# Routing in a mixture-of-experts layer: the first expert's rows picked with the one-hot matrix as loaded operand, row numbers and gates formed in another order

## The chip, the core and the metric

The kernel runs on one core of a Trainium2 chip. Its engines are PE (matrix products), DVE (VectorE), ACT (ScalarE), POOL (GpSimd) and SP, which here only issues DMAs. The metric is the device time of one execution in microseconds. The profile comes from one such execution.

## The reference

It is an encoder of two layers over 512 tokens of 1024 features. Each layer has an attention mixer and then a mixture of 16 experts of which a router picks 2 for each token. What matters here is the end of the mixer and the start of the experts:

```python
h = layer_norm(DEEPNORM_ALPHA * h + mix, ln1_g[l], ln1_b[l])        # mix = o @ w_out[l]
...
scores = sigmoid(einsum('nd,de->ne', h, router_w))                  # 512 x 16
biased = (scores + router_bias).reshape(n, N_GROUPS, GROUP_SIZE)
group_sel = argmax(sum(top_k(biased, 2)[0], -1), -1)                # best of 4 groups
_, idx = top_k(where(in_group, biased, NEG_INF), 2)                 # 2 experts of that group
gates = sel / sum(sel, -1)
for e in range(N_EXPERTS):
    a = silu(h @ w_gate[e]) * (h @ w_up[e])
    y = y + dense_gates[:, e:e + 1] * (a @ w_down[e])
h = layer_norm(DEEPNORM_ALPHA * h + y, ln2_g[l], ln2_b[l])
```

## The kernel before

The 512 tokens are four tiles of 128 rows, `h[:, t]`. Weights stream in as pieces of 128x1024 (512 KB) that SP's queue loads in a fixed order (L324) as buffers come free. Most pieces are split into a rounded high part, made by ACT (L369), and a low part, made by DVE (L376) or POOL (L378). A product is then three matmuls (L400 to L402: high x high, low x high, high x low). The first piece of each expert matrix is kept whole and multiplied in full f32 (L1700), which the trace records as two PE rows for each matmul. `prep` makes high parts ahead of need as far as `prep_limit` and the buffer budget allow; `prep_low` makes the low parts.

`w_out_phase` ends the mixer. For each tile t it forms two halves of the output projection (`mm(t, 0)`, `mm(t, 1)`), which DVE adds to h out of PSUM (L1375). `stats` takes the sums: a square on ACT (L729), and POOL raises the variance to a power (L736). `tr` turns h by PE transposes (L1384), copied out by ACT and DVE (L1387). `logits` is 8 products with the router's 16 columns (L1396). `score` applies the norm to the logits afterwards (L1400, L1401) and ACT takes a tanh. `finish` makes the normed rows themselves, on DVE alone (L1407, L1408: `fast`) or on DVE and POOL (L1410 to L1412), and SP writes them to `hD` in DRAM. FIN = 13 makes tiles 0, 2 and 3 fast.

`choose(a, b)` finds the two experts of tiles a to b-1: a chain of some 14 short DVE instructions (L1502 to L1523). `places(a, b)` counts with small matmuls (L1532) which row of its expert each token takes, and DVE writes that number into `R1` (L1534). Rows of the experts from the second on are fetched from `hD` by an indirect DMA (L1619) at row numbers that `start(e)` forms from one-hots (L1587) and small matmuls (L1594).

The first expert's rows are not fetched. `pick(t)` makes a 128x128 one-hot of the tile (L1418) and multiplies: the loaded operand is a strided view of h (every eighth column), the moving operand the one-hot, and the result lands already transposed in two PSUM tiles `G`. `trans_x(0)` then only splits `G` into high and low parts (L1658 to L1660). `zero` opens and closes the sums in `G` with a product of zeros (L1424). `moe` follows with `proj(0, "g")` (the first expert's gate matrix), `start(1)`, `make_gates` (L1539 to L1549), `proj(0, "u")` and `trans_x(1)` (L1689), and so on for 16 experts.

Each engine runs its instructions in one order that a scheduler sets when the kernel is built, with semaphores between engines. `issue_after(i)` puts what is issued under it behind the instruction i on the same engine. `busy(n)` issues n small matmuls of zeros that nobody reads (L552), "dummies" below.

## Time and profile before

| | us |
|---|---|
| Median of 3 runs | 1386.37 |
| Lowest and highest of them | 1381.67, 1392.21 |
| The profiled execution's own time | 1383.48 |
| Its span, first to last instruction | 1381.7 |
| Mean granted PE clock, share of full speed | 0.978 |

The span is 1.8 us less than the execution's own time; that remainder lies around the instructions. The profiled execution lies 2.9 us under the median. The two layers run the same code, so each place of interest stands twice in the trace: at about 305 to 364 us and at about 968 to 1024 us.

### The profile page before, as it was taken

Reading aid. Unit: us, or ns where it says so; the run is one execution under the profiler, and the core shown is the slowest. Engines: PE = TensorE matmul, PEld = TensorE weight load, DVE = VectorE, ACT = ScalarE, POOL = GpSimd, SP = SyncE. Lnnn points to the kernel's source line nnn. Section 1 sums busy time; section 2 is a strip of 40 time slices with the busy share of each in tenths; the row PEclk is TensorE's granted clock in tenths of the full one; section 3 lists DMA queues with packets and bytes.
Section 4 is the critical chain, followed back from the end, with each engine's and each line's share of the span. In section 5 each row is a group of like instructions: output and inputs, shape, how many; then the busy total and the mean of one; then the engine's idle time right before and its main releaser. Section 6 shows DMA issues by size and latency. Waiting matters only on the chain. (4 is left out here: it accounts for less than half of the span.)

```text
span 1381.7 us, 18726 instructions
## 1 busy us (share of the span) xinstructions
PE 1295.2 (94%) x6034; PEld 959.4 (69%) x6042; DVE 1017.1 (74%) x2292; ACT 799.4 (58%) x1429; POOL 265.0 (19%) x204
## 2 busy tenths in 40 slices
PE   8999999989999999899799989999999999979994
PEld 4786666768777776577588766677877777656773
DVE  6668888676678777677755788867858877757775
ACT  5468756651566665566436776557246666555662
POOL 1012222342021210111000222214412111102110
PEclk9999999998999999999999999999999999999998
DMA  8311313257699998999610124224769999888991
GB/s 258 87 46 31 111 62 92 80 174 242 232 301 316 348 364 244 342 390 357 228 43 16 31 81 123 93 76 155 233 242 296 312 356 352 251 290 295 387 367 61
DMA packets 114969, 289.01 MB, mean 209 GB/s; under 512 B 20548, under 2 KB 43332, under 8 KB 114864
## 3 DMA queue, kind: packets, MB, share of 16 engines
q1 hardware_dynamic: 101740, 253.48, 52.3%
q0 software_dynamic: 11008, 31.36, 9.1%
q10 hardware_dynamic: 2116, 2.89, 0.7%
q8 instruction: 50, 0.82, 0.2%
q14 instruction: 55, 0.45, 0.1%
HBM read 267.09 MB, written 27.00 MB: 213 GB/s over the span
## 5 line engine op out<-in xcount | busy, mean ns | idle before, releaser
L369 ACT ACTIVATE slot<-arena 128x1024 fp32r<-128x1024 f32 (+3 forms) x147 | 127.5, 887 | 95.7 <-PE A L402 27.3
L376 DVE TENSOR_TENSOR slot<-slot,slot 128x1024 fp32r<-128x1024 f32 x105 | 128.2, 1224 | 60.8 <-ACT slot L369 58.0
L369 ACT ACTIVATE slot<-slot 128x1024 fp32r<-128x1024 f32 x111 | 117.2, 1059 | 95.5 <-PE A L402 35.9
L402 PE MATMUL S<-slot,rounded 128*128 128x512 f32 x368 | 148.5, 404 | 0.3 <-DVE slot L376 0.2
L402 PE MATMUL A<-slot,rounded 128*128 128x512 f32 x372 | 147.2, 396 | 0.0
L376 DVE TENSOR_TENSOR slot<-arena,slot 128x1024 fp32r<-128x1024 f32 (+2 forms) x101 | 112.7, 1120 | 39.2 <-ACT slot L369 36.6
L400 PE MATMUL S<-slot,rounded 128*128 128x512 f32 x316 | 137.0, 436 | 3.7 <-ACT rounded L771 1.3
L401 PE MATMUL S<-slot,rounded 128*128 128x512 f32 x316 | 125.8, 398 | 1.0 <-DVE rounded L1926 0.7
L400 PE MATMUL A<-slot,rounded 128*128 128x512 f32 x288 | 125.6, 436 | 1.0 <-ACT rounded L771 1.0
L1624 POOL DMA_INDIRECT yD<-arena,ix x28 | 46.9, 1674 | 406.4 <-ACT rounded L1659 194.8
L401 PE MATMUL A<-slot,rounded 128*128 128x512 f32 x288 | 114.0, 396 | 2.3 <-DVE rounded L772 2.3
L2042 ACT ACTIVATE arena<-arena,ast 128x256 f32<-128x256 f32 (+3 forms) x160 | 88.9, 557 | 34.7 <-DVE ast L2031 25.5
L378 POOL TENSOR_TENSOR slot<-arena,slot 128x1024 fp32r<-128x1024 f32 (+4 forms) x46 | 70.2, 1542 | 195.7 <-ACT slot L369 175.1
L369 ACT ACTIVATE rounded<-slot 128x1024 fp32r<-128x1024 f32 x70 | 74.1, 1059 | 45.8 <-PE A L401 25.5
L400 PE MATMUL S<-rounded,slot 128*128 128x512 f32 (+1 forms) x224 | 89.3, 400 | 0.0
L401 PE MATMUL S<-rounded,slot 128*128 128x512 f32 (+1 forms) x224 | 88.4, 395 | 0.0
L402 PE MATMUL S<-rounded,slot 128*128 128x512 f32 (+1 forms) x224 | 88.1, 393 | 0.0
L402 PEld LDWEIGHTS S<-slot,rounded 128*128 128x128 f32 x368 | 70.7, 192 | 16.7 <-DVE slot L376 1.1
L2073 ACT ACTIVATE slot<-T 128x128 fp32r<-128x128 f32 (+3 forms) x128 | 53.4, 431 | 48.6 <-PE T L2068 47.7
L402 PEld LDWEIGHTS A<-slot,rounded 128*128 128x128 f32 x372 | 70.6, 190 | 15.4
L1700 PE MATMUL A<-slot,arena 128*128 128x512 f32 x168 | 79.4, 594 | 0.5 <-ACT arena L1658 0.5
L400 PEld LDWEIGHTS S<-slot,rounded 128*128 128x128 f32 x316 | 60.6, 192 | 21.7 <-issue 2.9
(371 smaller groups left out, 3061.8 us busy)
## 6 DMA issues: line engine op xcount, KB each, us to landing
slot<-in_exp_w_down_dram SPq DMA_DIRECT2D x80, 512.0 KB
slot<-in_exp_w_up_dram SPq DMA_DIRECT2D x73, 512.0 KB
slot<-in_exp_w_gate_dram SPq DMA_DIRECT2D x72, 512.0 KB
arena<-in_exp_w_gate_dram SPq DMA_DIRECT2D x60, 512.0 KB
arena<-in_exp_w_up_dram SPq DMA_DIRECT2D x59, 512.0 KB
arena<-in_exp_w_down_dram SPq DMA_DIRECT2D x52, 512.0 KB
arena<-in_w_in_dram SPq DMA_DIRECT2D x14, 512.0 KB
slot<-in_w_in_dram SPq DMA_DIRECT2D x12, 512.0 KB
```

The lines of the kernel that those rows point to most:

```text
L369: self.nc.scalar.activation(hi, r, AF.Copy)
L376: self.nc.vector.tensor_sub(lo, r, hi.bitcast(F32))
L378: self.nc.gpsimd.tensor_tensor(lo, r, hi.bitcast(F32), OP.subtract)
L400: t.matmul(ps, xh, wh, start=start, stop=False)
L401: t.matmul(ps, xl, wh, start=False, stop=False)
L402: t.matmul(ps, xh, wl, start=False, stop=stop)
L1624: self.nc.gpsimd.indirect_dma_start(out=self.yD[:, :], out_offset=bass.IndirectOffsetOnAxis(ap=ix[:, 0:1], axis=0), in_=y, in_offset=None, ...
L1700: nc.tensor.matmul(ps, xW(e)[:, kk], P.raw.f[:, 512 * k:512 * k + 512], start=kk == 0, stop=kk == 7)
L2042: nc.scalar.activation(p, p, AF.Exp, bias=self.st[:, m:m + 1], scale=-1.0, accum_out=self.st[:, 2 + m:3 + m])
L2073: nc.scalar.activation(self.part(0), self.ps, AF.Copy)
```

## The change

- `pick(t)`: the one-hot is now the loaded operand, and the contiguous row of h (two halves of 512) moves; two matmuls for each tile in place of eight. The result is the picked rows, not turned. `zero` is gone. `trans_x(0)` therefore copies the two tiles `G` to SBUF (ACT and DVE) and turns them by 8 PE transposes like those of any other expert, and then splits.
- `choose`, `places` and `pick` take tiles 0 to 2 in one go, tile 3 apart. `centre(3)`, the first half of the last `finish`, stands ahead of that, the second half behind the choice of tile 3.
- `finish(0)` is issued behind the copy of tile 1's transposes; before, it stood ahead of that tile's sums.
- No expert weight is split during `w_out_phase` (`prep_limit`), and low parts are held back (`hold_low`) until `G` is copied; the first expert's splits thus move from the end of the attention to the routing and the first gate.
- `start(1)`, which forms the second expert's row numbers, stands ahead of `trans_x(0)`, and `make_gates` between the two halves of the first gate projection.
- 3 dummies stand between the last tile's transposes and 13 behind its logits.

```diff
+WARM5 = 3
+WARM6 = 13
...
     def prep_low(self, n):
+        if self.hold_low:
+            return
         while self.i_low < n:
...
+        self.prep_limit = max(ids) + 1
         P = [self.get(i) for i in ids]
...
+        def centre(t):
+            z = self.h[:, t]
+            v.scalar_tensor_tensor(z, z, st[t][:, 1:2], self.lnrow[0], op0=OP.add, op1=OP.mult)
...
-        def pick(t, ks=range(8)):
+        def pick(t):
             oh = ho.f[:, 128 * t:128 * (t + 1)]
-            if ks[0] == 0:
-                v.tensor_scalar(oh, self.biota, self.R1[:, t, 0:1], None, op0=OP.is_equal)
-            hk = self.h[:, t].rearrange("p (d k) -> p k d", k=8)
-            for k in ks:
-                nc.tensor.matmul(self.G[k // 4][:, 128 * (k % 4):128 * (k % 4 + 1)], hk[:, k], oh, start=False, stop=False)
-
-        def zero(g, start):
-            nc.tensor.matmul(self.G[g], self.bzero, self.cum3, start=start, stop=not start)
+            v.tensor_scalar(oh, self.biota, self.R1[:, t, 0:1], None, op0=OP.is_equal)
+            for n in range(2):
+                i = nc.tensor.matmul(self.G[n], oh, self.h[:, t, 512 * n:512 * n + 512], start=t == 0, stop=t == NT - 1)
+            return i
...
                 if t == 1:
-                    finish(0, FIN & 1)
-                finish(t, FIN >> t & 1)
-            if t == 2:
-                self.choose(0, 2)
-        self.choose(2, 3)
+                    with self.tc.issue_after(self.i_trv.ins):
+                        finish(0, True)
+                finish(t, t == 2)
...
         tr(3, 0)
-        for g in range(2):
-            zero(g, True)
-        self.places(0, 2)
+        with self.tc.issue_after(self.i_tr.ins):
+            self.busy(WARM5, True)
         tr(3, 1)
-        pick(0, range(4))
-        pick(0, range(4, 8))
         scored(3)
-        finish(3, FIN >> 3 & 1)
-        pick(1)
+        with self.tc.issue_after(self.i_logit.ins):
+            self.busy(WARM6, True)
+        self.choose(0, 3)
+        centre(3)
+        self.places(0, 3)
+        for t in range(3):
+            pick(t)
         self.choose(3, 4)
-        self.places(2, 3)
-        pick(2, range(4))
         self.places(3, 4)
-        pick(2, range(4, 8))
+        with self.tc.issue_after(self.i_chosen.ins):
+            finish(3, True)
...
-        with self.tc.issue_after(self.i_chosen.ins):
+        self.prep_limit, self.hold_low = len(self.pieces), True
+        with self.tc.issue_after(self.i_score.ins):
             self.prep()
-        for g in range(2):
-            pick(3, range(4 * g, 4 * g + 4))
-            zero(g, False)
+        pick(3)
...
             if e == 0:
-                for half, ps in enumerate(self.G):
-                    hi, lo = [xT(0, s)[:, 4 * half:4 * half + 4] for s in range(2)]
-                    i = parts(ps.rearrange("p (k n) -> p k n", k=4), None if half else xW(0), hi, lo)
-                return i
+                x = B(gb[0]).f
+                nc.scalar.activation(x[:, 0:512], self.G[0], AF.Copy)
+                i = v.tensor_copy(x[:, 512:1024], self.G[1])
+                self.hold_low = False
+                with self.tc.issue_after(i.ins):
+                    self.prep_low(self.idx[l, "g0", WG] + 1)
+                self.hold_low = True
...
+        start(1)
         i_x = trans_x(0)
         pg[0] = self.psA.tile([128, 512], F32, name="A")
         proj(0, "g", pg[0], 0, 2)
         with self.tc.issue_after(i_x.ins):
-            start(1)
+            self.make_gates()
...
         with self.tc.issue_after(i_x.ins):
-            self.make_gates()
             gt[1] = self.slot_gates(self.slots(1, ohs.pop(1)))
```

Line numbers of the changed kernel run up to 14 higher than those used here. Three places of the built order follow, in the first layer; the second layer has the same ones.

**First place.** POOL at the end of the attention, before: three low parts of the first expert (L378), then the powers (L736) of tiles 0 and 1, with a low part of the attention's output (L1328) between them.

```order
L378 TENSOR_TENSOR slot8_2817<-arena_77,rounded_78 128x1024
L378 TENSOR_TENSOR slot14_2825<-arena_77,slot3_2824 128x1024
L378 TENSOR_TENSOR slot4_2820<-arena_77,slot1_2819 128x1024
L736 TENSOR_TENSOR bst_2861<-bst_2861,mhalf_82 128x1
L1328 TENSOR_TENSOR rounded_78<-slot5_1010,rounded_78 128x256
L736 TENSOR_TENSOR bst_2919<-bst_2919,mhalf_82 128x1
L1411 TENSOR_TENSOR h_73<-h_73,arena_77 128x1024
```


POOL at the same place now (L741 is the power, L1333 the attention's low part):

```order
L1333 TENSOR_TENSOR rounded_78<-slot5_1010,rounded_78 128x256 x2
L741 TENSOR_TENSOR bst_2847<-bst_2847,mhalf_82 128x1
L1333 TENSOR_TENSOR rounded_78<-slot5_1010,rounded_78 128x256
L741 TENSOR_TENSOR bst_2905<-bst_2905,mhalf_82 128x1
L1422 TENSOR_TENSOR h_73<-h_73,arena_77 128x1024
```


The three splits ahead of the first power are gone from POOL. DVE there, before: L1407 and L1408 are `finish(0)`, L1375 adds the second half of tile 1 to h, L1400 and L1401 are the scores of tile 0, and L1387 copies transposes of tile 0 (first row) and tile 1 (last row).

```order
L1387 COPY arena_77<-T_2887 128x512
L735 TENSOR_SCALAR bst_2861<-bst_2861 128x1
L1407 SCALAR_TENSOR_TENSOR h_73<-h_73,bst_2861,arena_77 128x1024
L1408 SCALAR_TENSOR_TENSOR h_73<-h_73,bst_2861,arena_77 128x1024
L1375 SCALAR_TENSOR_TENSOR h_73,zsum_2815<-S_2893,h_73 128x512
L1400 SCALAR_TENSOR_TENSOR sc_2816<-gbrw_2226,bst_2861,T_2907 128x16
L721 TENSOR_TENSOR bst_2919<-zsum_2815 128x1
L1401 SCALAR_TENSOR_TENSOR sc_2816<-sc_2816,bst_2861,gbrw_2226 128x16
L723 TENSOR_SCALAR bst_2919<-bst_2919 128x1
L1387 COPY arena_77<-T_2931 128x512
```


DVE there now (L1381 adds to h, L1406 and L1407 are the scores, L1412 and L1419 `finish(0)`):

```order
L1393 COPY arena_77<-T_2873 128x512
L1381 SCALAR_TENSOR_TENSOR h_73,zsum_2815<-S_2879,h_73 128x512
L1406 SCALAR_TENSOR_TENSOR sc_2816<-gbrw_2226,bst_2847,T_2893 128x16
L726 TENSOR_TENSOR bst_2905<-zsum_2815 128x1
L1407 SCALAR_TENSOR_TENSOR sc_2816<-sc_2816,bst_2847,gbrw_2226 128x16
L728 TENSOR_SCALAR bst_2905<-bst_2905 128x1
L1393 COPY arena_77<-T_2917 128x512
L1412 SCALAR_TENSOR_TENSOR h_73<-h_73,bst_2847,arena_77 128x1024
L1419 SCALAR_TENSOR_TENSOR h_73<-h_73,bst_2847,arena_77 128x1024
```


`finish(0)`, whose second half waits for POOL's power, moved from ahead of tile 1's addition to behind the copy of its transposes.

**Second place.** PE from the last picks to the first gate, before: L1421 picks, L1424 closes `G`, L1700 is the whole piece of the gate, L400 to L402 the split ones.

```order
L1421 MATMUL A_2832<-arena_77,h_73 128x128 x4
L1421 MATMUL A_2831<-arena_77,h_73 128x128 x4
L1424 LDWEIGHTS b_zero_92
L1424 MATMUL A_2831<-cum3_86,b_zero_92 128x512
L1421 MATMUL A_2832<-arena_77,h_73 128x128 x4
L1424 LDWEIGHTS b_zero_92
L1424 MATMUL A_2832<-cum3_86,b_zero_92 128x512
L1700 MATMUL A_3226<-arena_77 128x512 x2
L400 MATMUL A_3226<-rounded_78 128x512
L401 MATMUL A_3226<-rounded_78 128x512
```


PE there now: L1430 picks tile 3, L1599 are the last of the small matmuls for the second expert's row numbers, L1697 turns the picked rows, L1713 is the whole piece.

```order
L1599 LDWEIGHTS oh_e_3196
L1599 MATMUL T_3200<-mv_444,oh_e_3196 128x8
L1430 MATMUL A_2817<-h_73,arena_77 128x512
L1430 MATMUL A_2818<-h_73,arena_77 128x512
L1599 LDWEIGHTS oh_e_3198
L1599 MATMUL T_3200<-mv_444,oh_e_3198 128x8
L1697 MATMUL T_3218<-cst_72,arena_77 128x128 x4
L1697 MATMUL T_3226<-cst_72,arena_77 128x128 x4
L1713 MATMUL A_3236<-arena_77 128x512 x2
L404 MATMUL A_3236<-rounded_78 128x512
L405 MATMUL A_3236<-rounded_78 128x512
```


Eight transposes stand between the last pick and the gate, and the second expert's row numbers ahead of both.

**Third place.** DVE behind the last one-hot of tile 3, before: L1534 writes the row numbers, L1418 makes the one-hot, L1660 makes the low parts of the picked rows, then one-hots for the second expert (L1587) and the gates (from L1539).

```order
L1534 SCALAR_TENSOR_TENSOR R1_3005<-T_3193,ohs_3006 128x16
L1418 TENSOR_SCALAR arena_77<-b_iota1_436,R1_3005 128x128
L1660 TENSOR_TENSOR rounded_78<-A_2831,rounded_78 128x256
L1660 TENSOR_TENSOR rounded_78<-A_2832,rounded_78 128x512
L1587 TENSOR_SCALAR oh_e_3238<-b_iota1_436,R1_3005 128x128
L1587 TENSOR_SCALAR oh_e_3240<-b_iota1_436,R1_3005 128x128
L1587 TENSOR_SCALAR oh_e_3242<-b_iota1_436,R1_3005 128x128
L1587 TENSOR_SCALAR oh_e_3244<-b_iota1_436,R1_3005 128x128
L1539 TENSOR_SCALAR sc_2816<-sc_2816 128x64
```


DVE there now: L1539 row numbers, L1428 the one-hot, L1592 a one-hot of the second expert, L1688 copies half of `G`, L1604 and L1613 belong to the second expert's row numbers, L380 is a low part of a weight piece, L1665 of the picked rows.

```order
L1539 SCALAR_TENSOR_TENSOR R1_3095<-T_3169,ohs_3096 128x16
L1428 TENSOR_SCALAR arena_77<-b_iota1_436,R1_3095 128x128
L1592 TENSOR_SCALAR oh_e_3198<-b_iota1_436,R1_3095 128x128
L1688 COPY arena_77<-A_2818 128x512
L1604 COPY sw_3205<-T_3200 128x6
L380 TENSOR_TENSOR rounded_78<-arena_77,rounded_78 128x1024
L1613 SCALAR_TENSOR_TENSOR sf_3207<-sw_3205,cst_72 128x1
L1665 TENSOR_TENSOR rounded_78<-T_3218,rounded_78 128x256
L1614 SCALAR_TENSOR_TENSOR ix_3208<-sw_3205,cst_72,sf_3207 128x1
L1665 TENSOR_TENSOR rounded_78<-T_3226,rounded_78 128x512
L380 TENSOR_TENSOR slot4_3184<-arena_77,rounded_78 128x1024
L380 TENSOR_TENSOR slot14_3187<-arena_77,slot3_3186 128x1024
```


The three low parts of the first gate's pieces stand among those of the picked rows now, and the gates behind them.

## Rows read from the trace of the kernel before

**Rows 1.** The page: PE's busy time, share of the span, instructions.

```profile
PE 1295.2 (94%) x6034; PEld 959.4 (69%) x6042; DVE 1017.1 (74%) x2292; ACT 799.4 (58%) x1429; POOL 265.0 (19%) x204
```

**Rows 2.** Windows by stage: busy time (x instructions) of each engine, PEclk, DMA.

```profile
core 0: us, PE busy (x) PEld busy (x) DVE busy (x) ACT busy (x) POOL busy (x), PEclk, DMA share, GB/s
304.77:329.12 24.35, 21.34 (x113) 18.34 (x113) 14.75 (x39) 4.16 (x10) 11.66 (x8) 0.86 0.52 171
329.12:350.61 21.49, 19.91 (x112) 19.32 (x112) 11.52 (x63) 3.63 (x7) 1.50 (x2) 0.92 0.82 288
350.61:363.90 13.29, 12.90 (x61) 8.42 (x60) 11.94 (x50) 6.72 (x7) 3.10 (x3) 1.00 0.65 220
968.45:987.98 19.53, 18.51 (x113) 16.20 (x112) 15.47 (x37) 3.80 (x8) 12.56 (x8) 1.00 0.57 174
987.98:1010.23 22.25, 20.35 (x112) 19.72 (x113) 11.82 (x65) 3.76 (x8) 1.50 (x2) 0.85 0.84 293
1010.23:1024.21 13.98, 12.90 (x62) 8.26 (x60) 12.80 (x51) 7.57 (x8) 4.11 (x3) 1.00 0.66 227
```

**Rows 3.** Timeline of PE, first and second layer: start, busy, [idle before <-releaser].

```profile
311.45 1.10 PE L1384 MATMUL T<-cst,h 128*128 128x128 f32 x4 [3.01 <-DVE sc L1400]
...
972.81 0.72 PE L1384 MATMUL T<-cst,h 128*128 128x128 f32 x4 [1.02 <-DVE sc L1400]
```

**Rows 4.** Windows of two stretches in the first layer.

```profile
310.65:317.40 6.75, 5.95 (x16) 4.88 (x17) 2.97 (x12) 1.37 (x3) 0.56 (x1) 0.50 0.78 277
334.55:337.85 3.30, 3.30 (x19) 3.30 (x17) 3.23 (x11) 0.22 (x1) 0.96 (x1) 0.50 0.71 248
```

**Rows 5.** Timeline of POOL and DVE, first layer.

```profile
302.66 5.73 POOL L378 TENSOR_TENSOR slot<-arena,slot 128x1024 fp32r<-128x1024 f32 x2
...
308.95 1.75 DVE L1408 SCALAR_TENSOR_TENSOR h<-h,bst,arena 128x1024 f32<-128x1024 f32 x1 [2.81 <-POOL bst L736]
```

**Rows 6.** Timeline of PE, first layer, from the last logits to the first gate.

```profile
332.63 1.96 PE L1396 MATMUL T<-rg,arena 128*128 128x16 f32 x16 [0.77 <-DVE R L1534]
...
334.54 4.06 PE L1421 MATMUL A<-arena,h 128*128 128x128 f32 x16
338.44 0.25 PE L1532 MATMUL T<-oh,bones_all 128*128 128x16 bf16 x4
...
338.64 5.96 PE L1421 MATMUL A<-arena,h 128*128 128x128 f32 x24
...
350.61 1.88 PE L1700 MATMUL A<-arena 128*128 128x512 f32 x4
```

**Rows 7.** One line's instructions: min/median/max ns, first and last start.

```profile
L1421 PEld LDWEIGHTS A<-arena,h x128: 312/335/338, 334.5 to 1009.6; 128*128 128x128 f32 x128
```

**Rows 8.** Chain that ended last: start, length, what.

```profile
1271.47 1.72 PE A L1700 x4
```

**Rows 9.** Timeline of PE, first layer: the second expert's transposes; dummies.

```profile
363.90 1.04 PE L1689 MATMUL T<-cst,arena 128*128 128x128 f32 x8
...
681.61 0.65 PE L552 MATMUL A<-mchunk,b_zero 128*1 128x384 bf16 x3
```

**Rows 10.** Timeline of DVE, first layer.

```profile
321.11 1.69 DVE L721 TENSOR_TENSOR bst<-zsum 128x1 f32<-128x1 f32 x1
...
329.40 0.67 DVE L1375 SCALAR_TENSOR_TENSOR h<-S,h 128x512 f32<-128x512 f32 x1
...
334.86 1.28 DVE L1407 SCALAR_TENSOR_TENSOR h<-h,bst,arena 128x1024 f32<-128x1024 f32 x1
...
338.06 0.17 DVE L1502 SCALAR_TENSOR_TENSOR rt<-sc,rb 128x16 f32<-128x16 f32 x1
...
341.04 0.26 DVE L1522 TENSOR_TENSOR oh<-cst,rt 128x16 bf16<-128x16 f32 x2
...
362.27 1.22 DVE L376 TENSOR_TENSOR rounded<-slot,rounded 128x1024 fp32r<-128x1024 f32 x1
```

**Rows 11.** Timeline of PE, second layer: the second expert's transposes.

```profile
1024.21 1.14 PE L1689 MATMUL T<-cst,arena 128*128 128x128 f32 x8 [0.89 <-DMA arena<-hD,ix]
```

More of the change, by code (lines that the diff above doesn't have):

```diff
@@ L546, in setup, with busy @@
         self.pump()
-    def busy(self, n):
-        ps = self.psA.tile([128, 512], F32, name="A")
+    def busy(self, n, small=False):
+        ps = self.psS.tile([128, 512], F32, name="S") if small else self.psA.tile([128, 512], F32, name="A")
         for _ in range(n):
@@ L1406, in finish @@
             if fast:
-                v.scalar_tensor_tensor(z, z, st[t][:, 1:2], self.lnrow[0], op0=OP.add, op1=OP.mult)
+                if t < NT - 1:
+                    centre(t)
                 v.scalar_tensor_tensor(z, z, st[t][:, 4:5], self.lnrow[1], op0=OP.mult, op1=OP.add)
@@ L1690, in trans_x @@
                 hi, lo = [xT(e, s)[:, 4 * half:4 * half + 4] for s in range(2)]
-                parts(ps, None if half else xW(e), hi, lo)
+                i = parts(ps, None if half else xW(e), hi, lo)
+            if e == 0:
+                self.hold_low = False
+                with self.tc.issue_after(i.ins):
+                    self.prep_low(self.i_prep)
+            return i
         def proj(e, c, ps, j0, j1, then=None):
```

9 lines of the change are left out of this document (5 added, 4 removed).

## The prediction

> **What bounds the kernel now.** I read the page first: PE is busy 94% of the span [rows 1], so a change pays where PE is not doing needed work. Then I cut the place of the change into three stages for each layer [rows 2]. Stage A runs from the first logits to the end of the output projection, stage B from the last tile's transposes to the first gate product, stage C from there to the second expert's transposes. They take 24.35, 21.49 and 13.29 us in the first layer, 19.53, 22.25 and 13.98 us in the second. The same instructions stand in both, so the differences are waits and clock.
>
> In stage A the timeline shows one stall in each layer, 3.01 and 1.02 us, in front of tile 1's transposes, which wait for the score of tile 0 [rows 3]. DVE could not give that score: it stood in `finish(0)`, whose second half waited 2.81 us for POOL's power, and POOL was busy for 5.73 us with two weight splits queued ahead of it [rows 5]. Behind the long stall PE's granted clock fell to 0.50, which is 1.2 GHz, for 6.75 us [rows 4]; PE was busy for 5.95 us of those, so some 3.0 us were lost. That accounts for the first layer: 24.35 less 19.53 is 4.8, against 2.0 of longer stall and 3.0 of clock.
>
> In stage B, PE is nearly always busy (19.9 of 21.5 us), and the picks are most of it: the 64 rows from 334.54 to the gate at 350.61 [rows 6]. Their pace is 0.24 us a row at either clock: 16 rows in 3.9 us where the clock was 0.50 [rows 4], 24 in 5.96 where it was full. What sets it is the load of the strided operand, 335 ns [rows 7]. Stage C is PE-bound in the first layer (12.90 of 13.29 us) and loses 0.89 us in the second, waiting for the gather of the second expert's rows [rows 11].
>
> Behind stage C I count every microsecond as kept. PE is the bound there, and SP's queue waits mostly for the splits that free its buffers, so an earlier start shifts the loads as well.
>
> **Stage A.** The three splits leave POOL's queue and `finish(0)` stands behind the score, so neither can hold it. What is late next is PE itself: the second layer without its 1.02 us gives 18.5 us for both. Gain 5.85 + 1.0. A new neighbour is tile 1's `finish`, two products on POOL, under which DVE's short sums for tile 2 now fall. A one-column addition once took 1.69 us [rows 10]. Queued behind such a wait are the copy of tile 2's transposes and the logits on PE. The wait costs between nothing (it ends before PE arrives) and 1.7 us a layer; I take 0.6, since PE has ten matmuls in hand there.
>
> The Trainium skill's page "SBUF — State Buffer", section "Who interferes with whom", says that the one contention on the engines' side is a pair of ports that VectorE and GpSimd share under an exclusive lock. The 1.69 us addition agrees with that; by the rule each of these sums could wait for a whole GpSimd product, which is the upper end already taken.
>
> **Stage B**, counted from the first transposes of tile 3. Transposes, three dummies, transposes: 0.5 + 0.6 + 0.5, half of 1.04 us for 8 [rows 9] and 0.65 for three dummies; the eviction that the second half needs starts at 329.40, takes 0.67 [rows 10] and is over by 1.0. DVE's copy out of PSUM, 0.7, ends at 2.45. The second eight logit rows, half of 1.96 [rows 6], end at 3.5. From the score DVE needs the rest of three tiles' choice. One tile's whole chain took 3.2 us, from 338.06 to the end of the row at 341.04 [rows 10]; its first half is now done ahead of the score, three index searches stand in place of one, and `centre(3)` (1.28) is in it. I take 3.2 again: 6.7. The 13 dummies, 0.2 each, end at 6.1 and cost nothing as long as they end before that. 18 counting matmuls (eight took 0.2 between 338.44 and 338.64 [rows 6]) and their output: 7.4. Row numbers and the first one-hot: 7.9.
>
> A pick is now two f32 matmuls of 512 contiguous columns, with a contiguous load. Two of that form take 1.72 us [rows 8], so three tiles take 5.2: 13.1. Tile 3's choice and `finish(3)` run on DVE meanwhile (3.2 + 1.3 against 5.2). Counting, row number and one-hot of tile 3: 13.8. Its pick: 15.5. PSUM to SBUF, 0.7 + 0.2: 16.4. The new transposes and the eviction that the gate waits for: 1.2, between the 0.9 that 8 transposes take and the 1.6 from 363.90 to the next gate start where ACT was occupied. Stage B is 17.6 us, a gain of 3.9 and 4.65. The sum has eight hand-overs between engines at 0.1 or less each; for those I add back 0.8 a layer, ends 0 and 1.6.
>
> **Stage C.** The work on PE is 12.9 us in both layers [rows 2]. The gather is issued ahead of the gate in place of behind it, so its wait goes. New on DVE are three low parts, 1.22 each [rows 10], among those of the picked rows, with the gates behind them. Added up from the copy of `G` (six splits 7.3, copies and low parts 2.0, gates and row numbers 2.3) that is 11.6 us, and PE asks for the last gate column about 10.9 us after the copy (1.2 to the gate product, 5.9 for it, 3.8 into the up product). The 0.7 that PE may wait stands against small waits of 0.4 in the first layer that go. I take 12.9: gain 0.4 and 1.1. The three splits cost nothing only while PE works on the whole piece and its neighbours; without that cover they cost 3.7 us.
>
> **Clock.** In B, PE now idles for 0.6 us ahead of the counting and 0.5 behind it, with only small matmuls between. Such a stretch made a clock of 0.50 for 3.3 us in the first layer of before [rows 4]. There it cost nothing, since the strided loads set the pace; the new picks are paced by streaming and would lose half of it, 1.7 us. Whether the 13 dummies prevent it no row tells. The ends are 0 and a stretch like the 6.75 us one in each layer, 3.4 us lost in each; I take 1.7 once, in one layer of two.
>
> The Trainium skill's "TensorE: Matmul & The Clock Gate", section "What's actually happening", states that "the default state is throttled, and activity releases the throttle". By that rule the dummies are there for the picks, and the waiting on DVE that this change puts around them speaks against it; the trace agrees as far as the clock did fall behind the 3.01 us stall.
>
> **The sum.** Gains: 5.85 + 1.0 + 3.9 + 4.65 + 0.4 + 1.1 = 16.9 us. Taken back: ports 1.2, hand-overs 1.6, clock 1.7. Net 12.4 us. Against the profiled execution's own 1383.5 that is 1371.1; I say **1371 us**. That execution lies 2.9 us under the median; the stall of A differs from layer to layer, so slower executions may hold more of it, and I don't add the 2.9.
>
> **Rivals.**
> (a) Everything fits: no port wait, no slow stretch, hand-overs hidden. 1383.5 - 16.9 = 1366.6. For it: the dummies. Against it: eight hand-overs in a row.
> (b) DVE becomes the bound of B: three tiles chosen at once take not 3.2 but twice that, since the three finds stand in a row (3.2 us for one tile [rows 10]). PE waits another 3.2 us a layer: 1377.5. For it: DVE has 11.5 us of work in B already [rows 2]. Against it: instructions of three tiles can fill each other's gaps.
> (c) The clock stays at 0.50 through the picks in both layers, 3.4 lost in each: 1371.1 + 5.1 = 1376.2.
> (d) It doesn't do what it says in A: the score is still late, for another reason on DVE. Then A's 6.85 and its 1.2 drop out: 1376.7.
> (e) Slower: the clock falls at the waits behind the logits and stays at 0.50 to the end of the first gate. Paced by it are 13 dummies, four picks (6.9), the new transposes (0.9) and a gate (half of 12.9): 15.3 us lost a layer, 30.6 in all. In place of the 1.7 that gives 1400. It turns the sign when 7 us a layer are lost, 14 us in a row at 0.50; the longest stretch in these places is 6.75.
>
> **How the numbers follow.** The forecast 0.45, (a) 0.20, (b) 0.15, (c) 0.12, (d) 0.05, (e) 0.03. Bounds: 1366.6 at best; 1380 with the clock's 6.8, the ports' 3.4 and hand-overs of 3.2. The runs of before spread from 4.7 below their median to 5.8 above, so I open the lower end to 1363 and leave 1380. About 1% (14 us) is what a measurement of this kernel can tell from no change. Measured from the median that is 1372.5, from the profiled execution 1369.6; (a) lies past both, the forecast between them, so half of it counts. Faster 0.46, within 1% 0.50, slower 0.04.
>
> **What would show it.** Right: no stall ahead of L1390 (the tile transposes) in A; A 18.5 to 19.5 us in both layers; L1430 at 0.43 us a row where the clock is full; B near 18 and C near 13; the gather wait gone. Wrong: PE waiting over 2 us for L1527 or L1428 (rival b); a PEclk of 0.50 over the picks (c, e); a wait ahead of L1390 or L1402 on DVE (d, ports); or time given back in later experts, as waits on loads that I counted as shifted.

## The result

The changed kernel takes 1369.47 us in the median of 4 runs (1366.76 to 1374.33), the kernel before 1388.80 in its 4 (1381.67 to 1392.21). The ratio of the runs is 0.988, 95% interval 0.9858 to 0.9903, so 1.2% less (the two medians alone would give 0.986), where 1371 us and a range of 1363 to 1380 were forecast. The profiled execution took 1368.57 us, with a span of 1366.8, which is 14.9 under the 1381.7 of before.

The page's line of PE for the changed kernel, whose lines are numbered up to 14 higher:

```profile
PE 1285.1 (94%) x5986; PEld 937.6 (69%) x5986; DVE 1019.5 (75%) x2278; ACT 800.0 (59%) x1431; POOL 250.0 (18%) x196
```

The windows of its six stages, cut as in [rows 2]:

```profile
core 0: us, PE busy (x) PEld busy (x) DVE busy (x) ACT busy (x) POOL busy (x), PEclk, DMA share, GB/s
304.76:323.01 18.25, 18.25 (x114) 16.29 (x113) 12.59 (x31) 3.88 (x9) 6.80 (x4) 1.00 0.39 121
323.01:340.99 17.98, 15.24 (x89) 8.81 (x87) 13.17 (x64) 5.92 (x10) 1.50 (x2) 1.00 0.93 337
340.99:354.12 13.13, 12.78 (x56) 8.43 (x57) 12.20 (x37) 7.81 (x9) 1.94 (x1) 1.00 0.93 317
957.76:976.01 18.25, 18.25 (x113) 16.29 (x112) 12.59 (x31) 3.88 (x9) 6.81 (x4) 1.00 0.44 147
976.01:994.20 18.19, 15.26 (x90) 8.82 (x88) 13.18 (x64) 5.93 (x10) 1.51 (x2) 1.00 0.85 303
994.20:1007.33 13.13, 12.79 (x56) 8.43 (x57) 12.19 (x37) 7.78 (x9) 2.01 (x1) 1.00 0.93 329
```

Against [rows 2], A gains 6.10 and 1.28 us, B 3.51 and 4.06, C 0.16 and 0.85: 15.96 in all. PE is busy for the whole of A, and its clock is full in all six rows. Between the first layer's C and the second layer's A the changed kernel is 0.91 us shorter (603.64 for 604.55), behind the second C 1.98 longer (359.47 to the end for 357.49): 15.96 + 0.91 - 1.98 = 14.9.

PE in stage B of the first layer, from its timeline (start, busy, [idle before <-releaser]); L1402 are logits, L557 dummies, L1537 the counting, L1430 picks, L1697 the transposes of the picked rows, L1713 the gate:

```profile
324.73 2.01 PE L1402 MATMUL T<-rg,arena 128*128 128x16 f32 x16
326.67 2.27 PE L557 MATMUL S<-mchunk,b_zero 128*1 128x384 bf16 x13
329.70 0.18 PE L1537 MATMUL T<-oh,b_tri 128*128 128x16 bf16 x1 [0.76 <-DVE oh L1527]
...
330.90 5.42 PE L1430 MATMUL A<-h,arena 128*128 128x512 f32 x12 [0.54 <-DVE arena L1428]
...
336.98 1.98 PE L1430 MATMUL A<-h,arena 128*128 128x512 f32 x4 [0.55 <-DVE arena L1428]
...
339.83 1.13 PE L1697 MATMUL T<-cst,arena 128*128 128x128 f32 x8 [0.87 <-DVE sw L1604]
```

Three tiles are picked in 5.25 us, from 330.90 to the next product at 336.15, 0.44 a row. Four short waits for DVE are left, 2.7 us together. The load of the picks is contiguous now and takes 190 ns, as the line's own view says, against the 335 of [rows 7]:

```profile
L1430 PEld LDWEIGHTS A<-h,arena x32: 186/190/191, 330.9 to 991.1; 128*128 128x128 f32 x32
```

### The profile page after: what moved, and what is told of

Its sections match the earlier page's. It is cut to its first block, busy times and chain, and to the rows that moved or that the text cites. A ratio compares the mean times of both kernels' runs of the same rounds, so it can differ in the third digit from the quotient of the medians.

```text
span 1366.8 us, 18569 instructions
## 1 busy us (share of the span) xinstructions
PE 1285.1 (94%) x5986; PEld 937.6 (69%) x5986; DVE 1019.5 (75%) x2278; ACT 800.0 (59%) x1431; POOL 250.0 (18%) x196
## 5 line engine op out<-in xcount | busy, mean ns | idle before, releaser
L373 ACT ACTIVATE slot<-arena 128x1024 fp32r<-128x1024 f32 (+4 forms) x146 | 126.5, 886 | 100.7 <-PE A L406 32.8
L380 DVE TENSOR_TENSOR slot<-slot,slot 128x1024 fp32r<-128x1024 f32 x104 | 127.1, 1224 | 52.1 <-ACT slot L373 51.5
L380 DVE TENSOR_TENSOR slot<-arena,slot 128x1024 fp32r<-128x1024 f32 (+2 forms) x104 | 116.5, 1123 | 47.0 <-ACT slot L373 44.9
L1713 PE MATMUL A<-slot,arena 128*128 128x512 f32 x200 | 95.0, 594 | 0.5 <-ACT arena L1663 0.5
L382 POOL TENSOR_TENSOR slot<-arena,slot 128x1024 fp32r<-128x1024 f32 (+4 forms) x42 | 58.9, 1417 | 195.9 <-ACT slot L373 175.3
L406 PEld LDWEIGHTS S<-slot,rounded 128*128 128x128 f32 x368 | 70.3, 191 | 17.3 <-DVE slot L1910 1.9
L404 PE MATMUL A<-rounded 128*128 128x512 f32 x164 | 77.6, 473 | 0.0
```

Of the source, the lines that this page charges most:

```text
L373: self.nc.scalar.activation(hi, r, AF.Copy)
L380: self.nc.vector.tensor_sub(lo, r, hi.bitcast(F32))
L382: self.nc.gpsimd.tensor_tensor(lo, r, hi.bitcast(F32), OP.subtract)
L404: t.matmul(ps, xh, wh, start=start, stop=False)
L406: t.matmul(ps, xh, wl, start=False, stop=stop)
L1713: nc.tensor.matmul(ps, xW(e)[:, kk], P.raw.f[:, 512 * k:512 * k + 512], start=kk == 0, stop=kk == 7)
```

## The experiments

My theory was that the three stages gain each by its own mechanism: A by a score that nothing holds up, B by a cheaper pick in a chain that DVE sets, C by an earlier gather. The rivals were that one part made all of it, or that dummies and clock did. Twelve kernels follow; the table has their ratios to the kernel before and the stages of the profiled execution (first / second layer, us). One kernel's runs lie up to 12.6 us apart, so that what is smaller than some 4 us is read from the stages. The stages are those of one execution each; even the time ahead of the first A differs by 3.1 us between before and e4, whose code is the same up to there (A begins at 304.77 and at 301.65).

| kernel | ratio (95%) | A | B | C |
|---|---|---|---|---|
| before | 1 | 24.35 / 19.53 | 21.49 / 22.25 | 13.29 / 13.98 |
| changed | 0.988 (0.9858 to 0.9903) | 18.25 / 18.25 | 17.98 / 18.19 | 13.13 / 13.13 |
| e5 finish(0) first | 0.9916 (0.9896 to 0.9936) | 18.27 / 18.27 | 18.00 / 18.05 | 13.14 / 13.15 |
| e6 splits back | 0.9907 (0.9891 to 0.9923) | 18.36 / 18.25 | 18.89 / 20.47 | 12.47 / 12.46 |
| e12 finish(0) alone | 0.9961 (0.9939 to 0.9982) | 18.35 / 18.64 | 23.75 / 22.70 | 14.61 / 14.65 |
| e2 A's part alone | 1.0036 (1.0014 to 1.0058) | 18.25 / 18.26 | 26.47 / 27.11 | 14.55 / 15.63 |
| e9 no hold | 0.9989 (0.9971 to 1.0007) | 18.25 / 18.25 | 26.62 / 26.87 | 12.52 / 12.53 |
| e4 new pick alone | 0.9933 (0.9916 to 0.995) | 22.93 / 19.52 | 19.38 / 19.34 | 13.03 / 12.84 |
| e3 old pick | 1.0013 (0.9996 to 1.0031) | 18.25 / 18.25 | 27.02 / 27.11 | 12.69 / 12.69 |
| e10 row numbers, gates late | 0.998 (0.9962 to 0.9998) | 18.25 / 18.25 | 19.75 / 18.06 | 15.52 / 16.43 |
| e1 no dummies | 0.9906 (0.9887 to 0.9925) | 18.25 / 18.25 | 20.08 / 21.21 | 13.16 / 13.15 |
| e8 split choice | 0.9897 (0.9879 to 0.9915) | 18.26 / 18.25 | 18.14 / 18.15 | 13.16 / 13.15 |
| e11 the same, filled | 0.9886 (0.9863 to 0.9909) | 18.25 / 18.25 | 18.27 / 16.66 | 13.12 / 13.12 |
| e7 centre(3) late | 0.9878 (0.9855 to 0.99) | 18.25 / 18.25 | 16.89 / 16.89 | 13.15 / 13.16 |

### What ends A's stall: e5, e6, e12, e2

**e5**, the changed kernel with `finish(0)` in its old place:

```diff
                 if t == 1:
-                    with self.tc.issue_after(self.i_trv.ins):
-                        finish(0, True)
+                    finish(0, True)
```

> The changed kernel with finish(0) back in its old place, ahead of tile 1's addition; no expert weight is split during the output projection, as in the changed kernel. Theory 1 (the two halves of stage A's change are each enough: POOL free gives the power at once, so finish(0) waits for nothing and is done before the score is asked for): A 18.25 us as in the changed kernel, at most 0.5 us more, the whole time the same within 1 us. Rival (the place on DVE is what counts): the 2.6 us of finish(0) still stand ahead of tile 0's score, PE waits 1 us in front of tile 1's transposes as in the second layer of before, A 19.3 to 19.5 us in both layers, the whole 2 us longer.

**e6**, the changed kernel with the splits allowed again:

```diff
-        self.prep_limit = max(ids) + 1
...
-        self.prep_limit, self.hold_low = len(self.pieces), True
+        self.hold_low = True
```

> The changed kernel with the expert's splits allowed again during the output projection (three on POOL ahead of the power, as before); finish(0) stays behind the copy of tile 1's transposes, low parts stay held behind A. Theory 1 (the place on DVE alone takes the stall away, POOL is late but nobody on PE waits for it): A 18.3 to 18.8 us; since the first expert's splits are done early, C is 12.7 to 13.1, the whole within 1 us of the changed kernel. Rival (the score needs the power from POOL too, which three splits hold up): the score of tile 0 comes 2 to 3 us late, PE stalls for it in front of tile 1's transposes, the granted clock falls behind that, A 20 to 24 us in a layer, the whole 2 to 8 us longer than the changed kernel.

Theory 1 held for A in both: 18.27 and 18.25 to 18.36 us. Beside the other changes, each step by itself takes the stall away. (e5's ratio is a little higher than the changed kernel's, but the intervals overlap and the stages are the same.) In e6 C is 0.66 shorter, since three low parts are off DVE, but B is 0.9 and 2.3 longer. DVE and PE of e6, first layer, and the picks of the second:

```profile
321.54 1.22 DVE L380 TENSOR_TENSOR rounded<-slot,rounded 128x1024 fp32r<-128x1024 f32 x1
...
323.41 1.06 PE L1401 MATMUL T<-rg,arena 128*128 128x16 f32 x8 [0.41 <-DVE bst L740]
...
983.48 7.11 PE L1429 MATMUL A<-h,arena 128*128 128x512 f32 x12 [0.50 <-DVE arena L1427]
```

Another split on DVE (1.22 us) delays the copy of the transposes, the second half of the logits waits 0.41 and 0.46 us, and the clock falls to 0.50 in both layers, over the dummies in the first (3.64 us for 2.27) and over the picks in the second (7.11 us for 5.42).

**e12**, the kernel before with the new place of `finish(0)` alone:

```diff
                 if t == 1:
-                    finish(0, FIN & 1)
+                    with self.tc.issue_after(self.i_trv.ins):
+                        finish(0, FIN & 1)
```

> The kernel before with one step alone: finish(0) stands behind the copy of tile 1's transposes. Splits, picks, choice and all else are as before. Theory 1 (A's gain needs only that place, and it is kept, since the first expert's low parts stay early on POOL and lock nothing in B): A 18.25 to 18.4 us in both layers, B 21.2 to 22.5, C 13.2 to 14.2, the whole 5 to 8 us under the kernel before (ratio 0.994 to 0.996). Rival (what A gains, B gives back, as in the run with both steps of A: DVE's work that ran under A's stall now stands ahead of the choice, places come late, PE idles and the clock falls): A 18.3, B 24 to 27 us, the whole within 2 us of before or slower.

The ratio is at the edge of Theory 1's, and its interval lies below 1. In the profiled execution the rival has its share: of 6.9 us gained in A, B and C give back 4.7. PE in the first layer:

```profile
322.91 0.17 PE L1533 MATMUL T<-oh,b_tri 128*128 128x16 bf16 x1 [1.48 <-DVE oh L1523]
...
324.64 3.29 PE L1396 MATMUL T<-rg,arena 128*128 128x16 f32 x16 [0.77 <-DVE R L1535]
...
358.62 1.13 PE L1690 MATMUL T<-cst,arena 128*128 128x128 f32 x8 [1.50 <-DMA arena<-hD,ix]
```

PE waits 1.48 us for the choice of tiles 0 and 1 (0.71 before), the logits then run at half clock for most of their time (3.29 us, 1.96 before), and C ends with 1.50 us of waiting for the gather.

**e2**, the kernel before with both steps of A, so without early splits:

```diff
+        self.prep_limit = max(ids) + 1
...
                 if t == 1:
-                    finish(0, FIN & 1)
+                    with self.tc.issue_after(self.i_trv.ins):
+                        finish(0, FIN & 1)
...
+        self.prep_limit = len(self.pieces)
         with self.tc.issue_after(self.i_chosen.ins):
             self.prep()
```

> The kernel before with stage A's part of the change alone: no expert weight is split during the output projection, and finish(0) stands behind the copy of tile 1's transposes. Picks, choice and the order behind are as before. Theory 1 (A's gain stands by itself): A 18.3 us in both layers, B 21.5 to 22.3 and C 13.3 to 14, so a span some 7.4 us under the 1381.7 of before, 1374. Rival (what A gains the first expert loses, since its splits now come late and there is no held order for them): A 18.3, but C or the stretch behind it longer by 2 to 4 us a layer, and the span at 1378 to 1382.

A is 18.25, and what it gains is lost again, as the rival said, but not where it said. It expected the loss in C or behind; C is 1.3 and 1.7 us longer, and B, of which it did not speak, 5 us in each layer, so that the kernel is slower than before. The timelines of POOL, DVE and PE, first layer, show where:

```profile
324.35 2.34 POOL L378 TENSOR_TENSOR rounded<-arena,rounded 128x1024 fp32r<-128x1024 f32 x1 [3.09 <-ACT rounded L369]
...
324.45 2.25 DVE L721 TENSOR_TENSOR bst<-zsum 128x1 f32<-128x1 f32 x1
...
327.22 0.17 PE L1535 MATMUL T<-oh,b_tri 128*128 128x16 bf16 x1 [3.35 <-DVE oh L1525]
```

A split that is no longer made early is made now, on POOL; the one-column sum, elsewhere 0.15 us, lasts until POOL is done; the experts' one-hots behind it are late, PE idles 3.35 us (2.1 of them are that sum), and the clock falls for 6.83 us from 327.27 on.

### The hold and the early row numbers: e9, e10

**e9**, the changed kernel without the hold on low parts:

```diff
-        self.prep_limit, self.hold_low = len(self.pieces), True
+        self.prep_limit = len(self.pieces)
...
-                self.hold_low = True
```

> The changed kernel without the hold on low parts: as soon as the high parts of the first expert are made behind stage A, POOL may make their low parts, beside the choice on DVE, as it does where stage A's part stands alone. Theory 1 (the hold pays: a 2.4-us product on POOL locks DVE out of the port for one short sum, 2.25 us in that run, on the chain of stage B, and PE, which then idles, loses clock): B 20 to 23 us in one or both layers, against 18.0 and 18.2, the whole 3 to 9 us longer. Rival (the loss there came from the old order of choice, and the dummies cover a late sum): B at most 18.8, C shorter by up to 0.5 since three low parts are off DVE, the whole the same within 1.5 us.

Theory 1 held, at about twice its price: B is 8.6 and 8.7 us longer, and no gain is left that the runs can tell from none. DVE, POOL and PE in the first layer:

```profile
325.34 1.26 DVE L1412 SCALAR_TENSOR_TENSOR h<-h,bst,arena 128x1024 f32<-128x1024 f32 x1
...
326.76 2.34 DVE L1507 SCALAR_TENSOR_TENSOR rt<-sc,rb 128x16 f32<-128x16 f32 x1
329.02 0.17 DVE L1528 TENSOR_TENSOR ohs<-oh 128x48 bf16<-128x48 bf16 x1
329.13 2.29 DVE L1509 TENSOR_TENSOR rt<-rt 128x12 f32<-128x12 f32 x1
331.35 0.16 DVE L1510 TENSOR_TENSOR rt<-rt 128x8 f32<-128x8 f32 x1
331.42 2.30 DVE L1511 TENSOR_TENSOR rt<-rt 128x4 f32<-128x4 f32 x1
...
325.63 3.44 POOL L382 TENSOR_TENSOR rounded<-arena,rounded 128x1024 fp32r<-128x1024 f32 x1 [1.98 <-ACT rounded L373]
329.03 2.37 POOL L382 TENSOR_TENSOR slot<-arena,rounded 128x1024 fp32r<-128x1024 f32 x1
331.36 2.35 POOL L382 TENSOR_TENSOR slot<-arena,slot 128x1024 fp32r<-128x1024 f32 x1
...
334.27 7.69 PE L1430 MATMUL A<-h,arena 128*128 128x512 f32 x12 [6.83 <-DVE arena L1428]
```

Three short steps of tile 3's choice, otherwise 0.17 us each, end together with POOL's products; the row numbers of tiles 0 to 2 stand behind them in DVE's queue, and PE waits 6.83 us, after which the picks take 7.69 us for 5.42. The Trainium skill's "SBUF — State Buffer", section "Who interferes with whom", says that a VectorE instruction with two inputs in SBUF contends with a GpSimd instruction that reads SBUF, and that the ports which the two share are an exclusive lock; these rows agree, since the three steps have two inputs each and end with a product.

**e10**, the changed kernel with row numbers and gates in their old places:

```diff
-        start(1)
         i_x = trans_x(0)
...
         with self.tc.issue_after(i_x.ins):
-            self.make_gates()
+            start(1)
...
         with self.tc.issue_after(i_x.ins):
+            self.make_gates()
```

> The changed kernel with the second expert's row numbers and the gates formed in their old places (row numbers behind the first half of the first gate product's start, gates behind the second). Theory 1 (the gather of the second expert's rows is issued later and C ends with a wait for it, as in the second layer of before): a wait of 0.5 to 2 us for the gathered rows ahead of the second expert's transposes, C 13.6 to 15 us in both layers against 13.1, the whole 1 to 4 us longer. Rival (an earlier end of B brought the gather forward by itself, as in the run with the new pick alone, whose C was 13.0 and 12.8): no wait for the gather, C 12.8 to 13.3, the whole the same within 1 us; B shorter by up to 0.3, since the row number's products are off PE there.

C is 2.4 and 3.3 us longer, so the rival is out, but Theory 1 asked too little and has only a part of the cause. PE's timeline: the picks of the first layer, the end of its C, a place near the end of its experts, and the end of the second layer's C:

```profile
327.93 7.11 PE L1430 MATMUL A<-h,arena 128*128 128x512 f32 x12 [0.54 <-DVE arena L1428]
...
353.93 0.35 PE L1599 MATMUL T<-mv,oh_e 128*128 128x8 bf16 x8 [1.81 <-DVE mv L1552]
...
665.18 1.13 PE L1727 MATMUL T<-cst,arena 128*128 128x128 f32 x4 [5.81 <-DVE arena L1841]
...
1016.03 0.36 PE L1599 MATMUL T<-mv,oh_e 128*128 128x8 bf16 x8 [1.58 <-DVE mv L1552]
...
1018.48 0.88 PE L1697 MATMUL T<-cst,arena 128*128 128x128 f32 x3 [1.35 <-DMA arena<-hD,ix]
```

For the gathered rows PE waits 0.20 and 1.35 us, for the gates 1.81 and 1.58 (in the changed kernel 0.34), and for a one-hot 0.57 in each layer. The low parts stand on DVE ahead of row numbers and gates now: the second expert's row numbers are written 7.4 us into C, not 0.6. The edit moves both, so it doesn't price the row numbers alone. In e4, which holds nothing, the old places cost nothing (C 13.03 and 12.84). That speaks for the hold as what makes the early places necessary; a kernel with neither was not run.

Another 6.9 us go between this C and the second layer, 5.3 of them in the one wait at 665.18 (0.51 us in the changed kernel). In B of the first layer the picks took 7.11 us in place of 5.42, at half clock for a part of them, although PE's order up to them is the changed kernel's.

### The form of the pick: e4, e3

**e4**, the kernel before with the new pick alone (G copied and turned as in the change, without the clearing of a buffer that the copy makes superfluous; no dummies):

```diff
-            for k in ks:
-                nc.tensor.matmul(self.G[k // 4][:, 128 * (k % 4):128 * (k % 4 + 1)], hk[:, k], oh, start=False, stop=False)
+            for n in range(2):
+                nc.tensor.matmul(self.G[n], oh, self.h[:, t, 512 * n:512 * n + 512], start=t == 0, stop=t == NT - 1)
...
-        pick(2, range(4))
+        pick(2)
         self.places(3, 4)
-        pick(2, range(4, 8))
```

> The kernel before with the new form of the pick alone (one-hot loaded, h moving, G copied and turned); choice, places, finish(0), splits and the place of the row numbers are as before, without dummies. A as before (some 24 and 19.5 us, or whatever the stall is in this execution). Theory 1 (the form gives the gain of B): work falls by 8.7 of picks less 2.3 of copy and transposes, some of it opens waits for DVE's choice of tile 3: B 17.5 to 18.5 us, like the changed kernel, so a span 7 us under the 1381.7. Rival (the old order can't use it: the choice of tile 3 with finish(3) ahead of it, and the row number of tile 2 behind that, set the end of B, and PE waits): B 19.5 to 21 us, the span 2 to 4 us under before.

The time is Theory 1's, 9.3 us less (B and C give 6.4 of it in the profiled execution); B, at 19.4, is the rival's. What keeps B there is not the order alone but the clock. PE's timeline, first layer:

```profile
328.39 3.60 PE L1396 MATMUL T<-rg,arena 128*128 128x16 f32 x16 [0.77 <-DVE R L1523]
...
331.93 3.54 PE L1419 MATMUL A<-h,arena 128*128 128x512 f32 x4
```

The granted clock is 0.50 for 6.83 us from 328.30. Four rows of the new pick take 3.54 us there, 0.88 each, twice the 0.44 at full clock, where the strided form kept 0.24 at either [rows 4]. (That the strided load's 335 ns set this pace is argued: no run changes the load alone.) The new form is cheaper, but only it pays for a fallen clock.

**e3**, the changed kernel with the old pick (no copy of G, no transposes; the products of zeros and the clearing of the buffer that the copy made superfluous are back, and the hold ends with the split of G):

```diff
-            for n in range(2):
-                i = nc.tensor.matmul(self.G[n], oh, self.h[:, t, 512 * n:512 * n + 512], start=t == 0, stop=t == NT - 1)
+            hk = self.h[:, t].rearrange("p (d k) -> p k d", k=8)
+            for k in range(8):
+                nc.tensor.matmul(self.G[k // 4][:, 128 * (k % 4):128 * (k % 4 + 1)], hk[:, k], oh, start=False, stop=False)
...
-                if 0 < i < 2 or i > 9:
+                if i < 2 or i > 9:
```

> The changed kernel with the old form of the pick: h as the strided loaded operand, eight products of 128 columns for each tile, the result turned already, so no copy of G and no transposes in front of the first gate. The order of choice, places and dummies is the new one. Theory 1 (the form pays, since all four picks now stand in a row behind the choice): 64 rows at 0.244 us are 15.6 in place of 16 rows at 0.43, 6.9, so 8.7 us more, less the copy and transposes that go, some 2.3 us: B 24.4 us in both layers, 6.4 more than the changed kernel in each, a span of about 1380. Rival (the picks lie beside waits for DVE, so that their form hardly matters and the order made the gain): B at most 20 us, the span under 1371.

Theory 1, again with more: B is 9.0 and 8.9 us longer, not 6.4. DVE, POOL and PE, first layer:

```profile
328.09 1.14 DVE L1526 TENSOR_SCALAR rt<-rt,rt 128x4 f32<-128x4 f32 x2
...
328.26 0.95 POOL L1647 MEMSET arena<- 128x1024 f32 x1
...
332.82 11.71 PE L1431 MATMUL A<-arena,h 128*128 128x128 f32 x48 [0.54 <-DVE arena L1428]
```

64 rows at 0.244 us are there as forecast, 8.6 us more. The end is no shorter than the changed kernel's by more than 0.4 (1.6 from the last pick to the gate, against 2.0). And PE begins to count 7.64 us into B, not 6.69. Some 0.2 of these 0.95 us are there when the score begins (3.96 us into B, not 3.77; a product of zeros stands between the logits). The rest is the clearing on POOL, which falls into DVE's choice and under which a step of that choice lasts until it ends. The clearing is a second edit in this kernel, told apart by its own rows.

### Dummies and clock: e1, e8, e11

**e1**, the changed kernel without dummies:

```diff
-WARM5 = 3
-WARM6 = 13
+WARM5 = 0
+WARM6 = 0
```

> The changed kernel without the 16 dummies, all else kept. Theory 1 (the dummies only fill a wait for DVE, and the chain of DVE sets stage B): B stays at 18.0 to 18.2 us less the 0.65 us of the three dummies between the transposes, where DVE's copy can come sooner, so 17.4 us in both layers, granted clock 1.00 over the picks, and the whole time within 1.5 us of the changed kernel. Rival (the dummies hold the clock up): PE idles some 3 us behind the last logits, the granted clock falls to 0.50 over a part of the picks or the first gate for 3.4 us or more, and since the new picks are paced by streaming, B and C together get 1.7 us (one 3.4-us stretch) to 3.4 us (one of 6.8) longer in a layer, up to 7 us in all.

The rival held in the stages: B is 2.1 and 3.0 us longer. PE's wait and picks in the first layer, from its timeline:

```profile
328.86 0.20 PE L1537 MATMUL T<-oh,b_tri 128*128 128x16 bf16 x1 [3.32 <-DVE oh L1527]
...
330.04 7.37 PE L1430 MATMUL A<-h,arena 128*128 128x512 f32 x12 [0.49 <-DVE arena L1428]
```

The windows of the slow stretches in both layers:

```profile
327.18:334.01 6.83, 4.66 (x23) 2.45 (x24) 6.02 (x31) 2.75 (x3) 0.00 (x0) 0.50 0.86 325
...
982.53:992.77 10.24, 6.91 (x26) 3.18 (x27) 7.18 (x43) 3.06 (x4) 0.49 (x1) 0.50 0.80 280
```

PE idles 3.32 us where the dummies stood, the clock falls to 0.50 in both layers of the profiled execution, and the picks of the first are slower by 1.95. The intervals of the two ratios overlap, so the whole shows this only in tendency. The Trainium skill's "TensorE: Matmul & The Clock Gate", section "What's actually happening", has the throttle as the default that activity releases; this run agrees.

**e8**, a version meant to be faster: tiles 0 and 1 are chosen early, and their picks stand where the 13 dummies were:

```diff
+            if t == 2:
+                self.choose(0, 2)
...
-            self.busy(WARM6, True)
-        self.choose(0, 3)
-        centre(3)
-        self.places(0, 3)
+            pick(0)
+            i = pick(1)
+        with self.tc.issue_after(i.ins):
+            self.busy(WARM6, True)
+        self.choose(2, 4)
+        self.places(2, 4)
```

> A version of the changed kernel meant to be faster: tiles 0 and 1 are chosen during the output projection as before, so their picks run beside the score and choice of tiles 2 and 3 in place of 13 dummies; 7 dummies stand behind these two picks. centre(3) and finish(3) stand behind the one-hots that they held up. Theory 1 (B is the chain transposes, logits, one choice, places, picks, and two of four picks leave it): logits end 3.6 us into B, the picks of two tiles at 7.1, the choice of two tiles at 8.5, their one-hots 9.4, their picks 12.9, copy and transposes 2.1: B 15 us, 3 less than the changed kernel in each layer, a span of 1361. Rival (DVE has no room for the first choice during the output projection, as in the run with stage A's part alone, where it ended 1.3 us late even without the port wait; places come late, PE idles and the clock falls): B 17.5 to 20 us, no gain.

B is 18.15, in the rival's range, but not for its reason: places came in time, and PE's waits ahead of the first picks are 0.21 and 0.41 us. These picks, from PE's timeline of the first layer:

```profile
324.72 5.38 PE L1433 MATMUL A<-h,arena 128*128 128x512 f32 x8
```

The clock fell to 0.50 as they began, the 8 rows took 5.38 us in place of 3.5, and the 7 dummies behind them held PE 1.4 us past the choice.

**e11**, the same with the two waits filled:

```diff
-WARM5 = 3
+WARM5 = 4
...
         with self.tc.issue_after(self.i_tr.ins):
+            self.busy(3, True)
             self.places(0, 2)
```

> The version with the choice split (tiles 0 and 1 chosen during the output projection) with PE's two short waits, 0.21 and 0.41 us, filled: 4 dummies in place of 3 between the transposes and 3 new ones behind them; the two one-hots stand ahead of the score. All else kept. Theory 1 (in that run only the clock took the gain: it fell to 0.50 as the first picks began, which cost 1.8 us on them and pushed the 7 dummies behind them 1.5 us past the choice): no fall, picks of tiles 0 and 1 in 3.5 us, B 16.2 to 16.6 us in both layers, 1.7 under the changed kernel's, the whole 3 us under it. Rival (the waits are not what the clock answers to, small products ahead of the picks are, and more dummies change nothing): PEclk 0.50 over the first picks again, B 18 us.

Each won one layer: B 18.27 in the first, with the fall again, and 16.66 in the second, without. PE's picks of the first, from its timeline:

```profile
324.63 5.38 PE L1433 MATMUL A<-h,arena 128*128 128x512 f32 x8
```

The windows of the slow stretch and of the second layer's B:

```profile
324.95:328.36 3.41, 3.41 (x5) 1.35 (x4) 3.24 (x15) 2.04 (x4) 0.00 (x0) 0.50 0.90 323
...
972.69:989.35 16.66, 15.09 (x88) 8.50 (x86) 13.29 (x62) 6.15 (x11) 1.50 (x2) 1.00 0.78 267
```

The instructions of B are the same in both layers, and in the first PE had no wait ahead of the fall that its timeline shows. So the clock does cost what was thought, 1.6 us, but filling the waits does not settle whether it falls.

### A faster version: e7

**e7**, the changed kernel with `centre(3)` behind the one-hots and 9 dummies for 13:

```diff
-WARM6 = 13
+WARM6 = 9
...
         self.choose(0, 3)
-        centre(3)
         self.places(0, 3)
         for t in range(3):
             pick(t)
+        with self.tc.issue_after(self.i_oh.ins):
+            centre(3)
```

> The changed kernel with centre(3) behind the one-hots of tiles 0 to 2 in place of between the index search and the experts' one-hots, and 9 dummies in place of 13. Theory 1 (DVE's chain sets B, and 1.26 us of centre(3) stand in it): PE starts to count 1.1 us sooner, B 16.9 us in both layers against 18.0 and 18.2, the granted clock 1.00 over the picks, the whole 2 us under the changed kernel. Rival (the fewer dummies let the clock fall, or centre(3) only moves the wait ahead of tile 3's pick): B 18 us or more, with a PEclk of 0.50 over picks or a PE wait of over 1.5 us ahead of tile 3's pick.

Theory 1 held to the tenth: B is 16.89 in both layers at a clock of 1.00, and PE's wait for the experts' one-hots is 0.35 us, not 0.76. From PE's timeline, first layer:

```profile
327.93 0.18 PE L1538 MATMUL T<-oh,b_tri 128*128 128x16 bf16 x1 [0.35 <-DVE oh L1528]
```

The whole, 1367.30 us and a ratio of 0.9878, is the lowest measured, but its interval doesn't part it from the changed kernel's; the stages do, by 2.3 us.

## Why the prediction was right

**The bound and stage A.** Right, 18.25 for 18.5. The price for ports, 0.6 a layer, was not paid: one short sum took 0.40 us, and no wait of PE follows it. The prediction gave both steps together; e5 and e6 show that either would do. The size of the gain hangs in part on the execution of before, though: e4, with the same code up to there, has the same stall (3.02 us), but a shorter slow stretch with it, and A is 22.93 there, 1.4 less.

**Stage B.** The chain came nearly as added up. In us from the first transposes, forecast and then first layer: dummies end 6.1 and 5.93, counting begins 6.7 and 6.69, first pick 7.9 and 7.89, three picks end 13.1 and 13.14, pick of tile 3 begins 13.8 and 13.97, gate 17.6 and 17.98. Eight hand-overs cost 0.4 and 0.6, not 0.8. Rival (b) is out: three tiles' choice took what was forecast for one, and PE waited 0.76 us for it.

**Stage C.** 13.13 for 12.9: PE waits 0.34 us for the gates. The gather's wait of the second layer is gone, as said.

**The clock.** 1.7 us were set down for one slow stretch over the picks; the profiled execution has none. Three kernels have PE's order of B up to the picks and, to 0.2 us, its waits in common (changed, e5, e10), six layers, and one of the six has the stretch, at 1.7 us (7.11 for 5.42). e6 has the same order with 0.4 us of waiting among the logits, and a slow stretch in both layers, in one of them over the picks and again 1.7 us. So the size was right. Whether one layer in two was the right chance, so few layers don't tell, and that the profiled execution has none may be luck. Rival (e)'s price doesn't come: even in e1, with 10.24 us at 0.50, B lost 3.0, not 15. (Its terms, 2.6 + 6.9 + 0.9 + 6.45, add up to 16.9, not to 15.3; only its own 30.6 and 1400 rest on that.)

**The sum.** Gains of 16.9 were forecast and 4.5 taken back. Measured: A gained 0.53 more than forecast; B, hand-overs included, 0.98 less than its gross gain, and C 0.49 less; of the 4.5 the ports and the clock cost nothing, and outside the stages 1.07 were lost. 12.4 + 0.53 - 0.98 - 0.49 + 4.5 - 1.07 = 14.9. "Every microsecond kept" was right to 1.07 of 15.96, and the time behind the second C has one more slow stretch than before (0.50 from 1225.89 to 1229.30 us, PE busy throughout), which is up to 1.7 of the 1.98 lost there.

**What it did not see.** It priced the hold as a cost (low parts on DVE, 3.7 us without cover) and the early row numbers as a gain, the gather's wait (0.89 us in the second layer). Both are conditions. Without the hold no gain is left that the runs can tell from none (0.9989). With row numbers and gates in their old places a sixth of it is left (0.998), though only 5.7 us of that loss lie in C. With the old pick nothing is left either (1.0013). A's two steps alone make the kernel slower (1.0036), the new pick alone gains a little over half (0.9933). The parts don't add up, which a sum over stages can't show.

## What to carry to other kernels

Ahead of a chain of short DVE steps, look at what POOL will be doing beside it: keep POOL's long products out of the chain, and then look at who has to make them instead and what now queues behind those. When parts are priced one by one, ask of each what happens to the others without it; leaving one out told more here than doing one alone. An operand form whose pace the clock doesn't change (here the strided load's, 0.24 us a row at either) is slow but loses nothing at half clock; the faster one takes twice as long there (0.88 us a row for 0.44).

## What was not expected of the hardware

A short DVE step with two inputs beside a POOL product lasted until the product's end (2.25 to 2.34 us in place of 0.15 or 0.17; e2, e9), and three in a row met one product each. A step with one input was not held: in the changed kernel one at 317.32 took 0.15 us under a product that ran from 315.46 to 317.86. The other way round, a product that began under a 1.26-us DVE step took 3.44 us for 2.37 (e9). A clearing on POOL that reads nothing held a step of DVE as well, for 0.95 us in place of 0.22. POOL and DVE of the changed kernel, first layer:

```profile
325.70 0.96 POOL L1640 MEMSET arena<- 128x1024 f32 x1 [6.35 <-ACT arena L734]
...
325.73 0.95 DVE L1519 TENSOR_SCALAR rt<-rt,rt 128x4 f32<-128x4 f32 x1
```

The granted clock fell in one layer and not in the other with the same instructions ahead of it, and without a wait of PE (e11). What decides it stays open: no run here tells it.
